# A decoder trunk's first chunk: the first weight block split ahead of the features' cast, the second tile's transposes ahead of all products, three warm-ups in place of six

## The chip, the core and the metric

The kernel runs on one core of one Trainium2 chip. The core has five engines with a queue of instructions each: TensorE (PE; its weight loads, which overlap its products, are listed as PEld), VectorE (DVE), ScalarE (ACT), GpSimd (POOL) and SyncE (SP). Each works through its own queue in order and meets the others at semaphores. Loads are issued from SP's queue here and carried out by 16 DMA engines. The metric is the time of one execution on the device in microseconds (us).

## What is computed

Two layers of a decoder trunk on 256 tokens of width 1024, all in float32. Each layer adds four things to the residual x: half of a SwiGLU feed-forward block, a mixer of two kinds of attention heads, a cross attention, and half of a second SwiGLU block. Only the first feed-forward block of the first layer is touched here:

```
def rms_norm(x, w):
    y = x * lax.rsqrt(jnp.mean(x * x, axis=-1, keepdims=True) + EPS)
    return y * w

def swiglu(h, w_gate, w_up, w_down):
    return (jax.nn.silu(h @ w_gate) * (h @ w_up)) @ w_down

x = x + 0.5 * swiglu(rms_norm(x, ffn1_norm[l]), ffn1_w_gate[l], ffn1_w_up[l], ffn1_w_down[l])
```

w_gate and w_up are 1024 x 2816, w_down is 2816 x 1024.

## The kernel before

**Products in three parts.** TensorE multiplies numbers of a reduced form of float32 (fp32r). Each operand is therefore split in two: a rounded part "hi" and the remainder "lo", and each product is made of three: hi x hi, hi x lo, lo x hi, summed in the same PSUM bank. For weights, ACT writes hi (tile whi) and DVE lo (tile wlo); in the blocks of this chunk ACT multiplies by the norm's gain on the way (L153) and DVE subtracts (L154). For features, the 256 tokens are two tiles of 128 rows. PE transposes a tile of x into PSUM (four transposes of 128 x 128 make one tile "pt"), ACT casts it to hi (xfh, L369), DVE makes lo (xfl, L370).

**The weight stream.** All weights come in one planned list of transfers of 1 MB each (raw). Raw 0 and raw 1 are the two halves (weight rows 0 to 511 and 512 to 1023) of the first 512 columns of w_gate, raw 2 and raw 3 those of w_up, raw 4 and 5 the next gate columns, raw 6 and 7 the next up columns. There are three buffers (`rawp`, bufs=3), so raw 3 loads into raw 0's buffer once that is split, raw 4 into raw 1's, and so on. `fetch` (L128) issues them on SP; raw 0 and raw 1 are issued in four pieces each, with the quarters of x between them. A raw block of this part holds four weight blocks of 128 rows x 512 columns, each split into one whi and one wlo. `split_block` splits a single block (and fetches two transfers ahead on its first); `take` and `split` do the same for whole transfers, one ahead of the products that read them.

**The first chunk.** `first_chunk` (L482) computes the first 512 gate columns from x without its norm: the norm's gain is in the weights and its row factor is applied later by the silu (`silu`, L704, two ACTIVATE with scale rs). x arrives in quarters (tile t, half b), and raw 0 in pieces, so that the work can start early. `turn(t, b)` is four transposes, `put(pt, t, b)` the cast and the remainder, `part(kt, t, which)` one product of 128 x 512 for weight block kt, tile t and one of the three kinds (0 is xfh x whi, 1 is xfh x wlo, 2 is xfl x whi), and `block(kt)` all six of a weight block. `warm_up(n)` is n transposes of the identity whose result nobody reads; nine of them stand at the very start as well (L232).

**Order.** The block is written inside `in_order()`, which ties each instruction to the one before it on the same engine: the order in the text is the order on every engine. After the block the order comes from the framework's scheduler, which goes by the order of the text and by what its model of time holds ready, and by a planner in the kernel (`drive`), whose tasks give their cost by `yield`.

**After it.** `xstat` computes the first 512 up columns from raw 2 and raw 3 (L442 to L444). Then `silu` and `mult` (L709, DVE, once per tile) give silu(gate) x up; a task (`h_task`, L693, eight transposes "hp") transposes that 2.4 planner microseconds later, while `wstat` has begun the second gate chunk from raw 4 and raw 5.

Of the kernel before, what the change touches and what calls it, by code (L numbers as in the profile page):

```python
# [24 lines left out]
NT = S // P  # L25
# [20 lines left out]
def hymba_kernel(  # L46
# [19 lines left out]
    def nm(s):  # L66
        uid[0] += 1
        return f"{s}_{uid[0]}"

    def s4(shape, dt=F32, name="s4"):  # L70
        return sp.tile(shape, dt, name=nm(name), tag="s4")

    def small(cols, name="sc", rows=P, bufs=0):
        return sm.tile([rows, cols], F32, name=nm(name), tag=name, bufs=bufs or 4)

    def acc(name="acc"):
        return psa.tile([P, 512], F32, name=nm(name), tag="acc")

    def smp(name="smp"):
        return pss.tile([P, 512], F32, name=nm(name), tag="smp")  # L80
# [48 lines left out]
    def fetch(i):  # L129
        while len(raws) <= min(i, len(plan) - 1):  # L130
            src, nk, cw, _ = plan[len(raws)]
            r = rawp.tile([P, 4 * 520], F32, name=nm("raw"), tag="raw")
            rv = r[:, :nk * cw].rearrange("p (k c) -> p k c", k=nk)
            n = 4 if len(raws) < 2 else 1
            for k0 in range(0, nk, nk // n):
                nc.sync.dma_start(out=rv[:, k0:k0 + nk // n, :], in_=src[:, k0:k0 + nk // n, :])
                for t, j in ({0: [(1, 0)], 3: [(0, 1), (1, 1)]}.get(k0, []) if not raws else []):
                    load_x(t, j)
            raws.append(r)
# [5 lines left out]
    def split_k(i, sl, k, hi, lo):  # L145

        gk = plan[i][3]
        if gk is None:
            nc.scalar.copy(out=hi, in_=sl)  # L149
            nc.vector.tensor_tensor(out=lo, in0=sl, in1=hi.bitcast(F32), op=ALU.subtract)  # L150
        else:
            g = gcols[gk[0]][:, gk[1] + k:gk[1] + k + 1]
            nc.scalar.mul(hi, sl, g)  # L153
            nc.vector.scalar_tensor_tensor(out=lo, in0=sl, scalar=g, in1=hi.bitcast(F32), op0=ALU.mult,  # L154
                                           op1=ALU.subtract)

    def split_block(i, k):

        if k == 0:
            fetch(i + LA_D - 1)  # L160
            pieces.append([])
        cw = plan[i][2]
        if k % 2 == 0:
            slot[:] = [wp.tile([P, SLOT], F32R, name=nm(n), tag=n) for n in ("whi", "wlo")]
        sl = slice(k % 2 * cw, (k % 2 + 1) * cw)
        hi, lo = slot[0][:, sl], slot[1][:, sl]
        split_k(i, raws[i][:, k * cw:(k + 1) * cw], k, hi, lo)
        pieces[i].append((hi, lo))
        return [(hi, lo)]
# [30 lines left out]
    @contextmanager  # L200
    def in_order():

        traced = nc.cur_bb.bb.instructions
        n = len(traced)
        yield
        prev = {}
        for i in traced[n:]:
            if i.engine in prev:
                tc.add_manual_dep(i, prev[i.engine], mybir.DependencyInfo(mybir.DependencyClass.NoSync,
                                  mybir.DependencyReason.DATA), reason="in_order")  # L210
            prev[i.engine] = i.name
# [13 lines left out]
    def warm_up(n):  # L225
        for i in range(n):
            nc.tensor.transpose(warm[:, (i % 4) * P:(i % 4 + 1) * P], ident, ident)
# [113 lines left out]
    def inv_rms(ss, rs):  # L341
        ms = small(1, "ms")
        nc.vector.scalar_tensor_tensor(out=ms, in0=ss[:, 0:1], scalar=EPS, in1=ss[:, 1:2], op0=ALU.add, op1=ALU.add)
        nc.gpsimd.tensor_tensor(out=rs, in0=ms, in1=neghalf[:, 0:1], op=ALU.pow)  # L344

    def half(ap, j):
        return ap[:, j * 512:(j + 1) * 512]
# [20 lines left out]
    def put_split(hi, lo, src):  # L368
        nc.scalar.copy(out=hi, in_=src)  # L369
        nc.vector.tensor_tensor(out=lo, in0=src, in1=hi.bitcast(F32), op=ALU.subtract)  # L370
# [79 lines left out]
    def xstat(f, cw, ps):  # L450
        ps += [acc() for _ in range(NT)]
        for kb in range(2):
            pc = take()
            for j in range(4):
                c = 0.0
                for t in range(NT):
                    c += xmm(ps, f, 4 * kb + j, t, pc[j], cw)
                yield c
# [23 lines left out]
    def first_chunk(f, psa_, psb_):  # L482


        psa_ += [acc(), acc()]
        rs = [small(1, "rs0", bufs=2) for _ in range(NT)]
        sq = [s4([P, D], F32, "sq") for _ in range(NT)]
        sums = [small(2, "ss") for _ in range(NT)]
        pa = []

        def turn(t, b):
            pt = smp("pt")
            for j in range(4):
                kt = 4 * b + j
                nc.tensor.transpose(pt[:, j * P:(j + 1) * P], xs[:, t, kt * P:(kt + 1) * P], ident)
            return pt

        def put(pt, t, b):
            sl = slice(t * P, (t + 1) * P)
            put_split(f.h[b][:, :, sl], f.l[b][:, :, sl], pt.rearrange("p (k t) -> p k t", k=4))  # L500

        def part(kt, t, which):
            x = (f.hi, f.hi, f.lo)[which](kt, t)
            w = (pa[kt][0], pa[kt][1], pa[kt][0])[which]
            nc.tensor.matmul(psa_[t], lhsT=x, rhs=w, start=kt == 0 and which == 0, stop=kt == KT - 1 and which == 1)  # L505

        def block(kt, order=(0, 2, 1)):
            first = order[:2] if order[1] == 2 else order[:1]
            for t in range(NT):
                for w in first:  # L510
                    part(kt, t, w)
            for w in order[len(first):]:
                for t in range(NT):
                    part(kt, t, w)

        def squares(t):
            x = xs[:, t, :]
            nc.scalar.activation(sq[t][:, 0:512], half(x, 0), AF.Square, scale=1.0 / 32.0, accum_out=sums[t][:, 0:1])
            nc.vector.tensor_tensor_reduce(out=sq[t][:, 512:1024], in0=half(x, 1), in1=half(x, 1), scale=1.0 / 1024.0,
                                           scalar=0.0, op0=ALU.mult, op1=ALU.add, accum_out=sums[t][:, 1:2])  # L520

        with in_order():
            p0 = turn(0, 0)
            warm_up(6)
            put(p0, 0, 0)
            pa += split_block(0, 0)
            part(0, 0, 0)
            part(0, 0, 2)
            p1 = turn(1, 0)
            put(p1, 1, 0)  # L530
            part(0, 0, 1)
            for w in (0, 2, 1):
                part(0, 1, w)
            for kt in (1, 2):
                pa += split_block(0, kt)
                block(kt)
            pa += split_block(0, 3)
            p = [turn(t, 1) for t in range(NT)]
            block(3)
            pa += split_block(1, 0)  # L540
            for t in range(NT):
                put(p[t], t, 1)
            block(4, (0, 1, 2))
            for kt in (5, 6, 7):
                pa += split_block(1, kt - 4)
                if kt < 7:
                    squares(kt - 5)
                block(kt)
            taken[0] = 2
            for t in range(NT):  # L550
                inv_rms(sums[t], rs[t])
        yield 16 * T512
        yield from xstat(f, 512, psb_)
        rb = sq[0].rearrange("p (j t) -> p j t", j=8)
        pt = smp("rt")
        for t in range(NT):
            nc.vector.tensor_scalar(out=rb[:, t, :], in0=ident, scalar1=0.0, scalar2=rs[t], op0=ALU.mult, op1=ALU.add)
            nc.tensor.transpose(pt[:, t * P:(t + 1) * P], rb[:, t, :], ident)
        row = sm.tile([P, S], F32, name=nm("L"), tag="L", bufs=1)
        nc.vector.tensor_copy(out=row, in_=pt[:, 0:S])  # L560
        hrs = [small(1, "hrs0", bufs=2) for _ in range(NT)]
        for t in range(NT):
            nc.vector.tensor_scalar(out=hrs[t], in0=rs[t], scalar1=0.5, scalar2=None, op0=ALU.mult)
        return rs, hrs, row
# [634 lines left out]
```

## Time and profile before

| | |
|---|---|
| median of three runs | 1235.88 us (1235.5 to 1235.89) |
| profiled execution, own time | 1236.02 us |
| profiled execution, span of instructions | 1234.2 us |
| PE busy | 1222.1 us of the span |
| DVE busy | 770.2 us |
| ACT busy | 653.7 us |
| HBM traffic | 217.28 MB read, 177 GB/s over the span |

The profile is of one execution. Its own time is a little longer than the span from its first to its last instruction. The views used below are the page (summary), the timeline (instructions in order of time: start, duration, engine, line, operation, output<-inputs, shape, number merged, and in brackets the idle time of the engine ahead of it with what ended it), the table of stretches (busy time of each engine in a stretch, then the granted TensorE clock, the DMA engines' busy share and their GB/s), the load table (size and us from issue to landing) and the waits (who waited for whom: us in total, times, longest). A time quoted from the timeline is counted from the span's start. Matmuls are pipelined, so one that lasts 0.39 us can follow another after 0.23.

### The profile page before, as it was taken

Reading aid. Unit: us, or ns where it says so; the run is one execution under the profiler, and the core shown is the slowest. Engines: PE = TensorE matmul, PEld = TensorE weight load, DVE = VectorE, ACT = ScalarE, POOL = GpSimd, SP = SyncE. Lnnn points to the kernel's source line nnn. Section 1 sums busy time; section 2 is a strip of 40 time slices with the busy share of each in tenths; the row PEclk is TensorE's granted clock in tenths of the full one; section 3 lists DMA queues with packets and bytes.
Section 4 is the critical chain, followed back from the end, with each engine's and each line's share of the span. In section 5 each row is a group of like instructions: output and inputs, shape, how many; then the busy total and the mean of one; then the engine's idle time right before and its main releaser. Section 6 shows DMA issues by size and latency. Waiting matters only on the chain.

```text
span 1234.2 us, 21594 instructions
## 1 busy us (share of the span) xinstructions
PE 1222.1 (99%) x9053; PEld 1118.8 (91%) x9053; DVE 770.2 (62%) x1190; ACT 653.7 (53%) x1022; POOL 36.6 (3%) x52
## 2 busy tenths in 40 slices
PE   9999999999999999999999999999999999999997
PEld 7999888999889889998889998889998898999986
DVE  6966647588866665554474464475887766545643
ACT  7655435578754454444354453366686555443532
POOL 0000000001000000000000000000010000000000
PEclk9999999999999999999999999999999999999999
DMA  8655655643544375465374566465434533555740
GB/s 309 208 182 175 242 185 172 216 143 109 184 157 154 116 243 173 171 224 191 130 256 144 199 205 204 136 222 189 154 139 171 187 134 106 195 181 171 239 170 35
DMA packets 100290, 219.73 MB, mean 178 GB/s; under 512 B 4160, under 2 KB 16736, under 8 KB 100192
## 3 DMA queue, kind: packets, MB, share of 16 engines
q1 hardware_dynamic: 100032, 218.07, 52.3%
q8 instruction: 71, 1.16, 0.4%
q10 hardware_dynamic: 160, 0.27, 0.1%
q14 instruction: 27, 0.22, 0.1%
HBM read 217.28 MB, written 1.05 MB: 177 GB/s over the span
## 4 chain that ended last, share of the span: by engine, by line
PE 93%; DVE 4%; ACT 1%; POOL 1%; issue 1%; DMA 0%; POOLq 0%; ACTq 0%
PE acc L442 29%; PE acc L443 29%; PE acc L444 28%; DVE wlo L150 1%; PE pt L363 1%; PE acc L505 1%; PE al L771 1%; DVE wlo L154 1%; DVE xfl L370 0%; POOL rs L344 0%; POOL hrs L840 0%; DVE pp L899 0%; PE cpo L443 0%; PE cs L442 0%; PE cs L444 0%
## 5 line engine op out<-in xcount | busy, mean ns | idle before, releaser
L150 DVE TENSOR_TENSOR wlo<-raw,whi 128x1024 fp32r<-128x1024 f32 (+1 forms) x324 | 388.6, 1222 | 270.4 <-ACT whi L149 269.4
L149 ACT CAST whi<-raw 128x1024 fp32r<-128x1024 f32 (+1 forms) x324 | 330.5, 1048 | 275.1 <-PE acc L444 134.6
L442 PE MATMUL acc<-xfh,whi 128*128 128x256 f32 x1536 | 432.4, 282 | 0.0
L443 PE MATMUL acc<-xfl,whi 128*128 128x256 f32 x1536 | 430.7, 280 | 0.3 <-DVE xfl L370 0.2
L444 PE MATMUL acc<-xfh,wlo 128*128 128x256 f32 x1536 | 429.8, 280 | 0.0
L443 PEld LDWEIGHTS acc<-xfl,whi 128*128 128x128 f32 x1536 | 289.3, 188 | 0.9 <-DVE xfl L370 0.7
L444 PEld LDWEIGHTS acc<-xfh,wlo 128*128 128x128 f32 x1536 | 289.4, 188 | 0.0
L442 PEld LDWEIGHTS acc<-xfh,whi 128*128 128x128 f32 x1536 | 288.5, 188 | 0.8
L443 PE MATMUL acc<-wlo,hth 128*128 128x512 f32 (+1 forms) x352 | 136.2, 387 | 0.0
L442 PE MATMUL acc<-whi,hth 128*128 128x512 f32 (+1 forms) x352 | 136.0, 386 | 0.0
L444 PE MATMUL acc<-whi,htl 128*128 128x512 f32 (+1 forms) x352 | 135.6, 385 | 0.0
L442 PE MATMUL acc<-whi,xfh 128*128 128x512 f32 (+1 forms) x240 | 87.8, 366 | 0.0
L443 PE MATMUL acc<-wlo,xfh 128*128 128x512 f32 (+1 forms) x240 | 87.3, 364 | 0.0
L444 PE MATMUL acc<-whi,xfl 128*128 128x512 f32 (+1 forms) x240 | 87.1, 363 | 0.0
L444 PEld LDWEIGHTS acc<-whi,htl 128*128 128x128 f32 x352 | 66.2, 188 | 14.1
L442 PEld LDWEIGHTS acc<-whi,hth 128*128 128x128 f32 x352 | 66.1, 188 | 14.2
L443 PEld LDWEIGHTS acc<-wlo,hth 128*128 128x128 f32 x352 | 66.1, 188 | 13.9
L154 DVE SCALAR_TENSOR_TENSOR wlo<-raw,g,whi 128x512 fp32r<-128x512 f32 (+1 forms) x96 | 62.0, 702 | 19.9 <-PE acc L444 11.4
L153 ACT ACTIVATE whi<-raw,g 128x512 fp32r<-128x512 f32 (+1 forms) x96 | 58.1, 677 | 18.1 <-PE acc L443 14.4
L369 ACT CAST hth<-sil 128x512 fp32r<-128x512 f32 x36 | 22.3, 619 | 56.8 <-DVE sil L738 56.8
L444 PEld LDWEIGHTS acc<-whi,xfl 128*128 128x128 f32 x240 | 45.1, 188 | 7.6
L442 PEld LDWEIGHTS acc<-whi,xfh 128*128 128x128 f32 x240 | 45.1, 188 | 7.6
(271 smaller groups left out, 1553.5 us busy)
## 6 DMA issues: line engine op xcount, KB each, us to landing
raw<-in_ffn_w_down_dram SPq DMA_DIRECT2D x44, 1024.0 KB, 4.9
raw<-in_ffn_w_up_dram SPq DMA_DIRECT2D x40, 1024.0 KB, 5.2
raw<-in_ffn_w_gate_dram SPq DMA_DIRECT2D x38, 1024.0 KB, 5.2
raw<-in_w_in_dram SPq DMA_DIRECT2D x24, 1024.0 KB, 5.3
raw<-in_cross_wk_dram SPq DMA_DIRECT2D x8, 1024.0 KB, 5.3
raw<-in_cross_wv_dram SPq DMA_DIRECT2D x8, 1024.0 KB, 5.1
raw<-in_w_out_dram SPq DMA_DIRECT2D x8, 1024.0 KB, 4.9
raw<-in_cross_wq_dram SPq DMA_DIRECT2D x8, 1024.0 KB, 5.0
```

What stands on the lines that cost most here:

```text
L149: nc.scalar.copy(out=hi, in_=sl)
L150: nc.vector.tensor_tensor(out=lo, in0=sl, in1=hi.bitcast(F32), op=ALU.subtract)
L153: nc.scalar.mul(hi, sl, g)
L154: nc.vector.scalar_tensor_tensor(out=lo, in0=sl, scalar=g, in1=hi.bitcast(F32), op0=ALU.mult, op1=ALU.subtract)
L363: nc.tensor.transpose(pt[:, j * P:(j + 1) * P], hn[:, kt * P:(kt + 1) * P], ident)
L369: nc.scalar.copy(out=hi, in_=src)
L442: nc.tensor.matmul(ps, lhsT=lh, rhs=rh, start=start, stop=False)
L443: nc.tensor.matmul(ps, lhsT=lh, rhs=rl, start=False, stop=False)
L444: nc.tensor.matmul(ps, lhsT=ll, rhs=rh, start=False, stop=stop)
L505: nc.tensor.matmul(psa_[t], lhsT=x, rhs=w, start=kt == 0 and which == 0, stop=kt == KT - 1 and which == 1)
L771: nc.tensor.matmul(ps[s0:s0 + hb, c0:c0 + hb], lhsT=k[:, h, a:a + hb], rhs=rhs[:, h, a + step:a + step + hb], start=True, stop=True)
```

## The change

Only the start of the ordered block in `first_chunk` is rewritten:

```
         with in_order():
             p0 = turn(0, 0)
-            warm_up(6)
+            pa += split_block(0, 0)
             put(p0, 0, 0)
-            pa += split_block(0, 0)
-            part(0, 0, 0)
-            part(0, 0, 2)
+            warm_up(3)
             p1 = turn(1, 0)
             put(p1, 1, 0)
-            part(0, 0, 1)
-            for w in (0, 2, 1):
-                part(0, 1, w)
+            for t in range(NT):
+                for w in (0, 1, 2):
+                    part(0, t, w)
             for kt in (1, 2):
                 pa += split_block(0, kt)
                 block(kt)
```

The split of weight block 0 (L153 on ACT, L154 on DVE, and the issue of raw 2 on SP, which it contains) comes ahead of the cast and remainder of tile 0. Three warm-up transposes stand between the two tiles' transposes in place of six. The second tile's transposes come ahead of all six products of block 0; two of these stood ahead of them, one right behind. The products then go tile by tile in the order hi x hi, hi x lo, lo x hi. Nothing is computed that was not computed before.

## The prediction

> **What bounds the kernel now.** I read the page first: shares of busy time, then the chain that ended last.
>
> ```profile
> span 1234.2 us, 21594 instructions
> PE 1222.1 (99%) x9053; PEld 1118.8 (91%) x9053; DVE 770.2 (62%) x1190; ACT 653.7 (53%) x1022; POOL 36.6 (3%) x52
> PE 93%; DVE 4%; ACT 1%; POOL 1%; issue 1%; DMA 0%; POOLq 0%; ACTq 0%
> ```
>
> PE is busy for 1222.1 of 1234.2 us, so all stages together leave it 12.1 us of idle time; the change touches code of the first chunk alone. A table of stretches (us; then busy time per engine, PE first) says how much of the idle time lies there.
>
> ```profile
> 0.00:10.00 10.00, 7.69 (x31) 5.95 (x32) 3.55 (x10) 4.50 (x7) 0.70 (x6) 1.00 0.78 271
> 10.00:20.00 10.00, 10.00 (x49) 8.22 (x48) 8.02 (x17) 7.63 (x15) 1.40 (x2) 1.00 1.00 368
> ```
>
> In the first 10 us PE idles 2.3, from 10 to 20 not at all. The timeline of the first 10 us (start, us, engine, line; in brackets the idle time ahead and what ended it) shows what the ten are spent on.
>
> ```profile
> 4.01 1.12 PE L495 MATMUL pt<-ident,xs 128*128 128x128 f32 x4 [0.27 <-DMA xs<-in_x_dram]
> 4.92 1.49 PE L227 MATMUL warm<-ident 128*128 128x128 f32 x6
> 5.17 0.59 ACT L369 CAST xfh<-pt 128x512 fp32r<-128x512 f32 x1 [2.53 <-PE pt L495]
> 5.65 0.72 ACT L153 ACTIVATE whi<-raw,g 128x512 fp32r<-128x512 f32 x1
> 6.41 0.75 DVE L154 SCALAR_TENSOR_TENSOR wlo<-raw,g,whi 128x512 fp32r<-128x512 f32 x1
> 6.43 0.80 PE L505 MATMUL acc<-whi,xfh 128*128 128x512 f32 x1
> 7.02 0.50 PE L505 MATMUL acc<-whi,xfl 128*128 128x512 f32 x1
> 7.35 0.60 PE L495 MATMUL pt<-ident,xs 128*128 128x128 f32 x4
> 7.99 0.58 ACT L369 CAST xfh<-pt 128x512 fp32r<-128x512 f32 x1 [1.62 <-PE pt L495]
> 8.47 2.57 ACT L153 ACTIVATE whi<-raw,g 128x512 fp32r<-128x512 f32 x4
> 8.61 0.69 DVE L370 TENSOR_TENSOR xfl<-pt,xfh 128x512 fp32r<-128x512 f32 x1 [1.45 <-ACT xfh L369]
> 9.23 2.74 DVE L154 SCALAR_TENSOR_TENSOR wlo<-raw,g,whi 128x512 fp32r<-128x512 f32 x4
> 9.35 0.50 PE L505 MATMUL acc<-whi,xfl 128*128 128x512 f32 x1 [0.22 <-DVE xfl L370]
> 9.69 0.39 PE L505 MATMUL acc<-wlo,xfh 128*128 128x512 f32 x1
> 9.92 0.39 PE L505 MATMUL acc<-whi,xfh 128*128 128x512 f32 x1
> ```
>
> The last row is the first product of weight block 1; from there the products start 0.23 us apart (9.69 to 9.92). Ahead of it stands one path: transposes, warm-ups, cast and split, two products, the second tile's transposes (7.35), their cast (7.99), their remainder (8.61), the product at 9.35.
>
> **The change part by part.** I rebuild that stretch in the new order with these durations. For arrivals I take the load table narrowed to one issue each (last figure: us from issue to landing): weight piece 0, issued at 1.18, then x tile 1, issued at 1.65.
>
> ```profile
> raw<-in_ffn_w_gate_dram SPq DMA_DIRECT2D x1, 256.0 KB, 3.4
> ```
> ```profile
> xs<-in_x_dram SPq DMA_DIRECT2D x1, 256.0 KB, 3.8
> ```
> ```profile
> 1.18 0.42 SPq L136 DMA_DIRECT2D raw<-in_ffn_w_gate_dram  x1
> 1.65 0.42 SPq L143 DMA_DIRECT2D xs<-in_x_dram  x1
> ```
>
> *Split first.* Piece 0 is there at 1.18 + 3.4 = 4.58, so ACT makes whi at about 4.6 instead of 5.65, into time in which it idles now (2.53 us ahead of the cast). Four splits take 2.57, so one follows another after (2.57 - 0.72) / 3 = 0.62; the cast of tile 0 comes at 5.25 instead of 5.17 and ends at 5.84. Cost 0.08, covered, since no product can use it before the second tile's transposes are through. On DVE wlo runs from 5.4, xfl of tile 0 from 6.05 to 6.75. SP's issue of the next raw block, inside the split, is only emitted earlier; its place on SP's queue is the same.
>
> *Three warm-ups fewer, transposes moved up.* The four transposes at 4.01 hold PE for 4.92 - 4.01 = 0.91 us until the first warm-up starts, 0.23 each; with three warm-ups of the same shape PE gets to the second tile's transposes at 4.92 + 3 x 0.23 = 5.6, not 7.35. x tile 1 lands at 1.65 + 3.8 = 5.45, hardly ahead of that. Four transposes as long as those at 4.01 (1.12) end at 6.72. PE's queue behind them now holds all products: the one that ran at 6.43 goes after 6.6. That costs nothing where it counts, since what comes last is tile 1's chain: cast 6.76 to 7.34 (0.04 behind PE, as at 7.99), xfl 7.38 to 8.07, its product 8.11. The other five products, with inputs from 7.34 or earlier, fit between 6.6 and 8.11. Block 1 follows 9.92 - 9.35 = 0.57 later in the old order with one product between; now the waiting one is last of six, and the next comes 9.69 - 9.35 = 0.34 later: 8.45. ACT splits block 1 from 7.3 to 8.0, DVE till 8.8, and that remainder is needed by its fifth product only, 0.9 behind 8.45. **Gain at this point: 9.92 - 8.45 = 1.5 us**; between 1.2 (the six products at a slow pace) and 1.8 (tile 1's transposes at the quick pace, 0.3 sooner).
>
> *What is late next.* PE is then ahead of the old times by 1.5, and I look for the first thing it meets that is not. Within the first chunk it could be raw 1: the row at 8.47 is raw 0's last three blocks and raw 1's first, which was there by 8.47 + 3 x 0.62 = 10.3 and is now wanted at 9.1. If it lands no sooner than 10.3, ACT waits and ends its split at 11.0, with the casts of x's other half queued behind it; but those need transposes that PE reaches at 8.45 + 2 x 6 x 0.23 = 11.2, so this costs nothing. The next views are ACT, DVE, PE's weight loads and PE, from 20 to 36 us.
>
> ```profile
> 21.35 2.57 ACT L153 ACTIVATE whi<-raw,g 128x512 fp32r<-128x512 f32 x4 [1.43 <-DMA raw<-in_ffn_w_up_dram]
> 23.94 1.28 ACT L704 ACT_TABLE_LOAD   x1
> 25.23 1.27 ACT L704 ACTIVATE sil<-acc,rs 128x512 f32<-128x512 f32 x2
> 26.39 7.46 ACT L153 ACTIVATE whi<-raw,g 128x512 fp32r<-128x512 f32 x12
> ```
> ```profile
> 29.87 3.39 DVE L154 SCALAR_TENSOR_TENSOR wlo<-raw,g,whi 128x512 fp32r<-128x512 f32 x5
> 33.18 0.68 DVE L709 TENSOR_TENSOR sil<-sil,acc 128x512 f32<-128x512 f32 x1
> ...
> 34.11 0.67 DVE L709 TENSOR_TENSOR sil<-sil,acc 128x512 f32<-128x512 f32 x1
> ```
> ```profile
> 34.44 0.19 PEld L444 LDWEIGHTS acc<-xfh,wlo 128*128 128x128 f32 x1
> ```
> ```profile
> 35.03 1.03 PE L693 MATMUL hp<-ident,sil 128*128 128x128 f32 x8
> ```
>
> ACT waits 1.43 us for raw 3 (second half of the first up chunk, 21.3), and from there on it has no pause, for PE or anything else: four splits, table load, two silus, twelve splits. DVE's remainders follow these: the row at 29.87 is raw 5's four and raw 6's first, and behind it come the two L709, which end at 34.78. The eight transposes at 35.03 read what the two L709 write, four each. Now the landing of raw 3: issue on SP's queue, its load time, and what SP waited for just ahead of it.
>
> ```profile
> 12.40 0.38 SPq L136 DMA_DIRECT2D raw<-in_ffn_w_up_dram  x1
> ```
> ```profile
> raw<-in_ffn_w_up_dram SPq DMA_DIRECT2D x1, 1024.0 KB, 8.9
> ```
> ```profile
> SPq L136 <- DMA raw<-in_ffn_w_gate_dram: 0.3, 1, 0.3
> ```
>
> 12.40 + 8.9 = 21.3. Its buffer is raw 0's, whose last split ends at 9.23 + 2.74 = 11.97, but SP's last wait is for another load to land, not for DVE. Freeing raw 0 by 1.5 us sooner therefore moves nothing here. So the chain raw 3, splits, silu, splits, L709 stays where it is, and PE runs into it. With 1.5 in hand it comes to L693 at 33.5: it waits to 33.18 + 0.68 + 0.05 = 33.91 for the first four (0.05 from DVE's end to PE's start, as at 9.35), and to 34.83 for the other four, which started at 35.03 + 4 x 0.11 = 35.46 in before (eight take 1.03 and the four at 7.35 took 0.60, so 0.11 each). **0.6 us of the 1.5 is left**, less some 0.1 for starting up again: 0.5. It is all the same then whether the first stretch brings 0.8 or 1.8. Between, the products of the second gate chunk need the last remainder of raw 5, ready at 29.87 + 3 x 0.66 + 0.75 = 32.6 (0.66 = (3.39 - 0.75) / 4); the row at 34.44 is the first load that reads it, now at 32.9: just in time. After L693 both orders are the same with PE 0.5 ahead. DVE and ACT have more idle time there (62% and 53% busy over the span), and weight buffers are freed by PE itself, so I let the 0.5 reach the end.
>
> **The sum.** The profiled execution took 1236.02 us, 1.8 more than its span and 0.14 above the median of 1235.88. Less 0.5 it gives 1235.5; from the median, 1235.4, which is my forecast.
>
> **The rivals.**
> *The whole shift goes through* (1.5 us: 1234.4). It needs the L709 sooner: if, with the first chunk's products ending 1.5 sooner, the program's scheduler places the silus (with table load 2.55 us) ahead of raw 3's splits, in the 1.43 + 1.5 us in which ACT has nothing; or if it places L709 ahead of the fifth split of the row at 29.87 (0.66). For it: this part of the order is not written by hand, and L709 stands behind a split of raw 6 now. Against: both depend on the same early block, so their order should be kept. 22%.
>
> *Raw 3 lands later: the slower one* (1236.8). Raw 4 may load once raw 1 is split, now 1.5 us sooner, and may then share the DMA engines with the end of raw 3.
>
> ```profile
> 18.47 0.38 SPq L136 DMA_DIRECT2D raw<-in_ffn_w_gate_dram  x1
> ```
> ```profile
> raw<-in_ffn_w_gate_dram SPq DMA_DIRECT2D x1, 1024.0 KB, 5.5
> ```
>
> At the 368 GB/s of 10 to 20 us 1 MB moves in 2.8 us, so raw 4 starts 5.5 - 2.8 = 2.7 us after its issue: now at 17.0 + 2.7 = 19.7. Raw 3 has 1.6 us to go then; evenly shared it would take 1.6 longer. L693's second half would come at 34.83 + 1.6 = 36.4 against 35.46, 0.9 late. It decides from 0.6 us of delay on. Against: the landings of the two single-issue rows come in order of issue (4.58, then 5.45), an earlier load ahead of a later one. [...] 10%.
>
> *PE's slow pace lasts longer* (1236.8). In before four transposes took 1.12 at 4.01 and 0.60 at 7.35, 0.23 against 0.11 apart, at a granted clock of 1.00 in both rows of stretches (third figure from the end): PE doubled its pace some 3.3 us after the transposes began. If it takes 3.3 us from the products on instead, which now begin at 6.7, each product from 8.45 to 10 costs 0.46 and not 0.23: 1.55 / 0.46 = 3.4 products, 0.8 us, which the wait at L693 hides (1.5 - 0.8 is still 0.7). If it takes twice that, to 13.3, it is 10.5 products and 2.4 us, and PE is 0.9 behind before for good. [...] 4%.
>
> That the change does not do what it says is excluded on its own engines' orders, since the block is ordered by hand; what the scheduler does with all that comes after is not, and could shift waits anywhere: 14%, of which 6 beyond 0.2% to either side.
>
> **How the numbers follow.** Forecast 50%: 1235.1 to 1235.7 (first stretch or restart otherwise by 0.3). Whole shift 22%: 1234.0 to 1234.6. Raw 3 late 10%: 1235.9 to 1236.8. Slow pace 4%. Range 1234.0 to 1236.8. 0.2% is 2.5 us, about what a measurement of this kernel can tell from no change; no case that I can price reaches it. So faster 0.06, same 0.88, slower 0.06.
>
> **What would show it.** Right: whi of block 0 at 4.6; second tile's transposes at 5.6; block 1's first product at 8.45; ACT's splits of raw 3 still from 21.3; and a new wait of PE's hp transposes for DVE's L709 of about 0.9 us in two pieces. Wrong: no such wait with raw 3 unmoved, the silus ahead of raw 3's splits, or a block 1 that starts after 9.3.

## The result and the profile after

The changed kernel takes 1238.99 us (median of 7 runs, 1238.4 to 1240.04); the kernel before took 1235.88 in the same measurement (7 runs, 1235.35 to 1236.93). The ratio is 1.0024, 95% interval 1.0015 to 1.0033: slower by 3.1 us, where 1235.4 was forecast and "slower by over 0.2%" had a chance of 0.06. The profiled execution took 1238.72 us.

The page of the changed kernel, span and busy time:

```profile
span 1236.9 us, 21588 instructions
PE 1224.1 (99%) x9050; PEld 1120.0 (91%) x9050; DVE 771.2 (62%) x1190; ACT 653.9 (53%) x1022; POOL 36.7 (3%) x52
```

Against before the span is 2.7 us longer and PE's busy time 2.0 us longer, so PE's idle time has grown by 0.7 only. The time is not lost in waits. First the place where the change was made, in the timeline of the first 10 us (start, duration, engine, line; lines behind the block are 2 less than before):

```profile
3.93 1.11 PE L495 MATMUL pt<-ident,xs 128*128 128x128 f32 x4 [0.19 <-DMA xs<-in_x_dram]
4.69 1.28 ACT L153 ACT_TABLE_LOAD   x1 [4.69 <-DMA raw<-in_ffn_w_gate_dram]
4.84 0.72 PE L227 MATMUL warm<-ident 128*128 128x128 f32 x3
5.98 0.72 ACT L153 ACTIVATE whi<-raw,g 128x512 fp32r<-128x512 f32 x1
6.61 0.57 ACT L369 CAST xfh<-pt 128x512 fp32r<-128x512 f32 x1
7.04 0.66 PE L495 MATMUL pt<-ident,xs 128*128 128x128 f32 x4 [1.47 <-DMA xs<-in_x_dram]
7.73 0.59 ACT L369 CAST xfh<-pt 128x512 fp32r<-128x512 f32 x1 [0.56 <-PE pt L495]
8.35 0.69 DVE L370 TENSOR_TENSOR xfl<-pt,xfh 128x512 fp32r<-128x512 f32 x1 [0.26 <-ACT xfh L369]
9.10 0.50 PE L505 MATMUL acc<-whi,xfl 128*128 128x512 f32 x1
9.44 0.40 PE L505 MATMUL acc<-whi,xfh 128*128 128x512 f32 x1
```

Two rows are later than forecast. whi of block 0 comes at 5.98 and not at 4.6: ACT's table load (1.28 us) stands ahead of its first activation and waits with it for weight piece 0 (4.69). In before the first activation was the cast, its table load carried no such wait and ran in ACT's empty time:

```profile
1.36 1.28 ACT L369 ACT_TABLE_LOAD   x1 [1.36 <-PEq L1186]
```

And the second tile's transposes come at 7.04 and not at 5.6, since PE waits 1.47 us for x tile 1. In the load table narrowed to that one issue (last figure: us to landing) it took 5.3 us, against 3.8 in before, from the same place in SP's queue:

```profile
xs<-in_x_dram SPq DMA_DIRECT2D x1, 256.0 KB, 5.3
```

Block 1's first product starts at 9.44: 0.48 sooner than before's 9.92, not 1.5. Next the chain into which PE was to run. SP's queue, the load of raw 3, then ACT, DVE and PE from 20 to 36 us:

```profile
12.45 0.38 SPq L136 DMA_DIRECT2D raw<-in_ffn_w_up_dram  x1
13.07 0.33 SPq L338 DMA_DIRECT2D wn<-in_cross_norm_dram  x1
```
```profile
raw<-in_ffn_w_up_dram SPq DMA_DIRECT2D x1, 1024.0 KB, 7.7
```
```profile
20.18 2.57 ACT L153 ACTIVATE whi<-raw,g 128x512 fp32r<-128x512 f32 x4 [0.74 <-DMA raw<-in_ffn_w_up_dram]
```
```profile
32.93 0.68 DVE L707 TENSOR_TENSOR sil<-sil,acc 128x512 f32<-128x512 f32 x1
34.59 1.03 PE L691 MATMUL hp<-ident,sil 128*128 128x128 f32 x8
```

The scheduler has put raw 3 ahead of the norm's weights (512 KB), which stood ahead of it in before. Raw 3 landed 1.2 us sooner (7.7 us from its issue, 8.9 in before), ACT's splits of it start at 20.18 and not 21.35, the second silu product ends at 33.61, and the hp transposes (L691 now) wait for nothing at 34.59. At that point PE is 0.44 us ahead of before (35.03).

From there the lead is lost a little with every product. The two programs issue the same products in the same order after the first chunk, so each can be compared with itself in the other trace. Here is its start in the changed kernel less its start in the kernel before, both counted from the span's start:

```
at us:     53    133   253   373   493   613   733   853   973   1093  1213  last
offset:  -0.39 -0.04 +0.28 +0.37 +0.58 +1.00 +1.55 +1.84 +1.98 +2.15 +2.58 +2.69
```

That is 3.1 us over some 8,900 products, 0.35 ns each, and the largest lasting step is 0.1 us. The groups of PE's costliest lines say the same (busy time in us, then mean ns of one); before, then after:

```profile
L442 PE MATMUL acc<-xfh,whi 128*128 128x256 f32 x1536 | 432.4, 282 | 0.0
L443 PE MATMUL acc<-xfl,whi 128*128 128x256 f32 x1536 | 430.7, 280 | 0.3 <-DVE xfl L370 0.2
L444 PE MATMUL acc<-xfh,wlo 128*128 128x256 f32 x1536 | 429.8, 280 | 0.0
```
```profile
L442 PE MATMUL acc<-xfh,whi 128*128 128x256 f32 x1536 | 433.5, 282 | 0.0
L443 PE MATMUL acc<-xfl,whi 128*128 128x256 f32 x1536 | 431.4, 281 | 0.4 <-DVE xfl L370 0.2
L444 PE MATMUL acc<-xfh,wlo 128*128 128x256 f32 x1536 | 430.4, 280 | 0.0
```

Same counts, idle time ahead of them of 0.3 and 0.4 us in all, and 1.1 + 0.7 + 0.6 = 2.4 us more in these three groups. A product that waits for nothing has become slower, in lines that the change doesn't touch.

What differs there was found in the built programs. Behind the first chunk the order of every engine is the same (but for raw 3's issue), the mean granted clock is 0.999 in both, and every buffer has its old address but one kind. The split weights live in seven places each, whi and wlo, that are given out in turn. In before both go through their seven in the turn 0 6 5 4 1 2 3; in the changed kernel whi still does, while wlo goes 0 6 5 1 2 3 4. Four of seven remainders thus lie at another place beside the same whi, to the end of the program. That is the suspicion which the experiments test: **theory A**, the places of wlo set the pace of the products; **theory B**, the order of the first chunk, or the state in which it leaves PE, does.

### The profile page after: what moved, and what is told of

It is laid out like the page before. It is cut to its first block, busy times and chain, and to the rows that moved or that the text cites. A ratio compares the mean times of both kernels' runs of the same rounds, so it can differ in the third digit from the quotient of the medians.

```text
span 1236.9 us, 21588 instructions
## 1 busy us (share of the span) xinstructions
PE 1224.1 (99%) x9050; PEld 1120.0 (91%) x9050; DVE 771.2 (62%) x1190; ACT 653.9 (53%) x1022; POOL 36.7 (3%) x52
## 4 chain that ended last, share of the span: by engine, by line
PE 94%; DVE 3%; POOL 1%; ACT 1%; issue 1%; DMA 0%; SPq 0%; POOLq 0%; ACTq 0%
PE acc L442 29%; PE acc L443 29%; PE acc L444 29%; PE pt L363 1%; PE acc L505 1%; DVE wlo L150 1%; PE al L769 1%; DVE wlo L154 1%; DMA xs<-in_x_dram 0%; POOL hrs L838 0%; DVE pp L897 0%; PE cpo L443 0%; PE cs L444 0%; PE cs L443 0%; PE cs L442 0%
## 5 line engine op out<-in xcount | busy, mean ns | idle before, releaser
L442 PE MATMUL acc<-xfh,whi 128*128 128x256 f32 x1536 | 433.5, 282 | 0.0
L443 PE MATMUL acc<-xfl,whi 128*128 128x256 f32 x1536 | 431.4, 281 | 0.4 <-DVE xfl L370 0.2
L444 PE MATMUL acc<-xfh,wlo 128*128 128x256 f32 x1536 | 430.4, 280 | 0.0
L443 PEld LDWEIGHTS acc<-xfl,whi 128*128 128x128 f32 x1536 | 289.3, 188 | 1.0 <-DVE xfl L370 0.8
L442 PEld LDWEIGHTS acc<-xfh,whi 128*128 128x128 f32 x1536 | 289.5, 188 | 0.7
L444 PEld LDWEIGHTS acc<-xfh,wlo 128*128 128x128 f32 x1536 | 289.5, 188 | 0.0
L442 PE MATMUL acc<-whi,hth 128*128 128x512 f32 (+1 forms) x352 | 136.3, 387 | 0.0
L443 PE MATMUL acc<-wlo,hth 128*128 128x512 f32 (+1 forms) x352 | 136.2, 387 | 0.0
L444 PE MATMUL acc<-whi,htl 128*128 128x512 f32 (+1 forms) x352 | 136.1, 387 | 0.0
L442 PE MATMUL acc<-whi,xfh 128*128 128x512 f32 (+1 forms) x240 | 88.0, 367 | 0.0
L443 PE MATMUL acc<-wlo,xfh 128*128 128x512 f32 (+1 forms) x240 | 87.3, 364 | 0.0
L444 PE MATMUL acc<-whi,xfl 128*128 128x512 f32 (+1 forms) x240 | 87.2, 364 | 0.0
L444 PEld LDWEIGHTS acc<-whi,htl 128*128 128x128 f32 x352 | 66.2, 188 | 14.4
L443 PEld LDWEIGHTS acc<-wlo,hth 128*128 128x128 f32 x352 | 66.2, 188 | 14.2
L442 PEld LDWEIGHTS acc<-whi,hth 128*128 128x128 f32 x352 | 66.2, 188 | 14.2
L154 DVE SCALAR_TENSOR_TENSOR wlo<-raw,g,whi 128x512 fp32r<-128x512 f32 (+1 forms) x96 | 62.1, 705 | 22.9 <-PE acc L444 15.0
L153 ACT ACTIVATE whi<-raw,g 128x512 fp32r<-128x512 f32 (+1 forms) x96 | 58.2, 677 | 19.2 <-PE acc L443 15.1
L369 ACT CAST hth<-sil 128x512 fp32r<-128x512 f32 x36 | 22.3, 619 | 57.9 <-DVE sil L736 57.9
L444 PEld LDWEIGHTS acc<-whi,xfl 128*128 128x128 f32 x240 | 45.2, 188 | 7.7
L442 PEld LDWEIGHTS acc<-whi,xfh 128*128 128x128 f32 x240 | 45.1, 188 | 7.5
```

The source lines that it names most:

```text
L442: nc.tensor.matmul(ps, lhsT=lh, rhs=rh, start=start, stop=False)
L443: nc.tensor.matmul(ps, lhsT=lh, rhs=rl, start=False, stop=False)
L444: nc.tensor.matmul(ps, lhsT=ll, rhs=rh, start=False, stop=stop)
```

## The experiments

For each kernel the number that tells most is the growth of that same offset against the kernel before, from 53 us to the last product; it leaves out what the first chunk itself does. The table collects them; the turns are those of places.

```
kernel                       whi turn       wlo turn       at 53 us  last   growth
changed kernel               0 6 5 4 1 2 3  0 6 5 1 2 3 4   -0.39   +2.69   +3.1
after_warm6                  0 6 5 4 1 2 3  0 6 5 1 2 3 4   -0.66   +2.63   +3.3
after_xfirst                 0 6 5 4 1 2 3  0 6 5 1 2 3 4   +2.77   +5.82   +3.0
after_forced                 0 6 5 4 1 2 3  0 6 5 1 2 3 4   +5.35   +8.32   +3.0
before_slots                 0 6 5 4 1 2 3  0 6 5 1 2 3 4   +6.22   +9.56   +3.3
after_lolast                 0 6 5 4 1 2 3  0 6 5 4 1 2 3   -0.49   -0.57   -0.1
lolast_xfirst_table          0 6 5 4 1 2 3  0 6 5 4 1 2 3   +1.07   +0.62   -0.5
lolast_xfirst_table_warm6    0 6 5 4 1 2 3  0 6 5 4 1 2 3   +0.08   +0.42   +0.3
after_slots                  0 6 5 4 1 2 3  0 6 5 4 1 2 3   +5.13   +5.42   +0.3
before_forced                0 6 5 4 1 2 3  0 6 5 4 1 2 3   +4.66   +4.75   +0.1
after_both                   0 6 5 1 2 3 4  0 6 5 1 2 3 4   +5.33   +5.03   -0.3
after_whi                    0 6 5 1 2 3 4  0 6 5 4 1 2 3   +4.96   +4.83   -0.1
after_rot                    0 6 5 4 1 2 3  6 5 4 1 2 3 0   +3.66   +7.25   +3.6
```

Single pauses set the scatter of this number: where both turns are the old ones it runs from -0.5 to +0.3, and of the -0.5 of lolast_xfirst_table nearly all falls at one place, where PE in before pauses for 0.30 us (858.99) and here does not.

### Places given by hand, in both kernels

In place of one pool of seven buffers for each kind, seven pools of one buffer, taken in a written turn:

```
-    wp = ctx.enter_context(tc.tile_pool(name="wp", bufs=N_W))
+    wps = {n: [ctx.enter_context(tc.tile_pool(name=f"{n}{k}", bufs=1)) for k in range(N_W)] for n in ("whi", "wlo")}
+    turns = {"whi": [0, 6, 5, 4, 1, 2, 3], "wlo": [0, 6, 5, 1, 2, 3, 4]}
+    used = {"whi": 0, "wlo": 0}
...
+    def wtile(n):
+        k = turns[n][used[n] % N_W]
+        used[n] += 1
+        return wps[n][k].tile([P, SLOT], F32R, name=nm(n), tag=n)
...
-                lo = wp.tile([P, SLOT], F32R, name=nm("wlo"), tag="wlo")
+                lo = wtile("wlo")
```

**after_slots**: the changed kernel, both turns equal.

> The kernel after, with each whi and wlo tile put by name into one of seven fixed places, and wlo's places taken in the turn of the kernel before (0 6 5 4 1 2 3, the same as whi's). Theory A (wlo's places set the pace of the products): the products lose no more time against the kernel before than in its first 35 us, where the kernel after was 0.45 us ahead, so about 1235.5 us. Theory B (the loss comes with the order of the first chunk or the place of PE's instructions): as the kernel after, 1238.5 to 1239.5.

**after_forced**: the changed kernel, its own turns.

> Control for the run with wlo's places exchanged: the kernel after in the same way of writing, whi in the turn 0 6 5 4 1 2 3 and wlo in its own turn of the kernel after, 0 6 5 1 2 3 4. Both theories: as the kernel after, 1238.5 to 1239.5; under theory A some 3.3 us above the run with equal turns, under theory B the same as it.

**before_slots**: the kernel before, with the turns of the changed one.

> The kernel before with fixed places, wlo's taken in the turn of the kernel after (0 6 5 1 2 3 4), nothing else of the change. Theory A: slower by the 3.1 us that the products lost, 1238.5 to 1239.5. Theory B: as the kernel before, 1235.5 to 1236.5.

**before_forced**: the kernel before, its own turns.

> Control: the kernel before with fixed places and both turns as it has them (0 6 5 4 1 2 3). Both theories: 1235.5 to 1236.5; under theory A 3 us below the run with exchanged turns, under theory B the same as it.

Measured on one chip, beside 1236.43 for the kernel before: after_slots 1241.24 (ratio 1.0039, 1.0027 to 1.0052), after_forced 1244.58 (1.0063, 1.0051 to 1.0076), before_slots 1245.14 (1.0069, 1.0057 to 1.0082), before_forced 1241.37 (1.0041, 1.0027 to 1.0055). The differences are those of theory A: the exchanged turn costs 3.3 us in the changed kernel (1244.58 - 1241.24) and 3.8 in the kernel before (1245.14 - 1241.37), while at equal places the order of the first chunk changes 0.1 us (1241.24 against 1241.37). In the two programs built from the kernel before, the transfers' buffers (raw) come in another turn as well; before_forced, with a growth of 0.1 us, shows that this costs the products nothing. Theory B has nothing for the 3.8 in a kernel whose first chunk is the old one.

All four lie 5 to 6 us above what was expected of them, and the table says where: at 53 us they are already late by 4.7 to 6.2 us. Written this way, the program's scheduler places raw 2's splits ahead of the casts of x's second half. ACT and PE in before_forced (lines are 7 more there):

```profile
15.09 2.56 ACT L160 ACTIVATE whi<-raw,g 128x512 fp32r<-128x512 f32 x4 [3.97 <-DMA raw<-in_ffn_w_up_dram]
17.55 1.04 ACT L376 CAST xfh<-pt 128x512 fp32r<-128x512 f32 x2
```
```profile
18.17 1.28 PE L512 MATMUL acc<-whi,xfh 128*128 128x512 f32 x2 [2.95 <-ACT xfh L376]
```

ACT waits 3.97 us for a load with work standing behind it that could run, and PE waits 2.95 us for that work. So these four settle the pace, but not the sum.

### The same engines' orders, with the places restored

**after_lolast**: one line of the changed kernel, which sets only the order of block 0's six products on PE.

```
             for t in range(NT):
-                for w in (0, 1, 2):
+                for w in (0, 2, 1):
                     part(0, t, w)
```

In the built program it restores wlo's old turn; the orders of the four other engines are exactly those of the changed kernel.

> The changed kernel with block 0's products in the order hi x hi, lo x hi, hi x lo instead of hi x hi, hi x lo, lo x hi; nothing else is edited. In the built program this puts the remainders' seven buffers back to the same turn of places as the rounded parts' (0 6 5 4 1 2 3 for both), at the places of the kernel before; only four instructions of block 0 stand in another order on TensorE. Theory A (the place of wlo sets the pace of the products that load it): the offset of the product times against the kernel before stays at about -0.4 us from 26 us to the end, so 1235.5 us, some 3.3 under the changed kernel, within 0.2% of the kernel before. Theory B (the order of the first chunk, or which state it leaves PE in, sets the later pace): as the changed kernel, 1239, ratio 1.0024, offset growing by 3 us.

Measured: 1236.63 us (11 runs) beside 1236.22 for the kernel before (27 runs on the same chip): ratio 1.0005, 0.9996 to 1.0014, no difference. The profiled execution has a span of 1233.6 us, 0.6 less than before. The offset stays where the first chunk leaves it (-0.49, at the end -0.57). The three groups of after_lolast are those of before to 0.1 us:

```profile
L442 PE MATMUL acc<-xfh,whi 128*128 128x256 f32 x1536 | 432.4, 282 | 0.0
L443 PE MATMUL acc<-xfl,whi 128*128 128x256 f32 x1536 | 430.6, 280 | 0.3 <-DVE xfl L370 0.2
L444 PE MATMUL acc<-xfh,wlo 128*128 128x256 f32 x1536 | 429.8, 280 | 0.0
```

With the hand-placed pair this shows theory A: the change as a reordering is worth nothing that can be measured, and the 3 us come with the places that the allocator deals out, which hang on the order in which the first remainders are read.

### What about the places counts

Three kernels as after_forced, with another line of turns each (in this order: **after_both**, **after_whi**, **after_rot**); one profile of each, read by its growth.

```
-    turns = {"whi": [0, 6, 5, 4, 1, 2, 3], "wlo": [0, 6, 5, 1, 2, 3, 4]}
+    turns = {"whi": [0, 6, 5, 1, 2, 3, 4], "wlo": [0, 6, 5, 1, 2, 3, 4]}
+    turns = {"whi": [0, 6, 5, 1, 2, 3, 4], "wlo": [0, 6, 5, 4, 1, 2, 3]}
+    turns = {"whi": [0, 6, 5, 4, 1, 2, 3], "wlo": [6, 5, 4, 1, 2, 3, 0]}
```

> The changed kernel with fixed places, both turns exchanged alike (whi and wlo both 0 6 5 1 2 3 4). Read by the offset of the product times against the kernel before, 40 us against the last product; the fixed places' own 5 us lie ahead of that. Theory A1 (what counts is whether a wlo lies at the same place as its whi): no growth, as with both turns natural (+0.3). Theory A2 (wlo's own turn is a slow one, whatever whi does): growth of 3.1 us. Theory A3 (each combination of places of the weights that follow one another has a pace of its own): some other number.

> The changed kernel with fixed places, the turn of whi exchanged (0 6 5 1 2 3 4) and that of wlo natural (0 6 5 4 1 2 3): the mirror of the changed kernel. Growth of the offset from 40 us to the end: theory A1 (unequal places cost) +3 us; theory A2 (wlo's own turn) 0; theory A3 some other number, of either sign.

> The changed kernel with fixed places, wlo one step on in the same turn (whi 0 6 5 4 1 2 3, wlo 6 5 4 1 2 3 0): all seven pairs unequal instead of four of seven. Growth of the offset from 40 us to the end: theory A1 (unequal places cost) 7/4 of 3.1, 5.4 us; theory A2 (wlo's own turn) 0; theory A3 some other number, of either sign.

Measured: growth -0.3, -0.1 and +3.6 us (one execution each, of 1241.06, 1240.86 and 1243.28 us; 5.3, 5.0 and 3.7 of these are the lateness at 53 us that comes with the hand-given places). A1 (unequal places cost) falls by after_whi, which is as unequal as the changed kernel and costs nothing in sum, and by after_rot, which had 5.4 to come. A2 (wlo's turn as such) falls by after_both, where the changed kernel's turn of wlo costs nothing, and by after_rot, where the old turn, one step on, costs most. What is left is A3, that each combination has a pace of its own. The spacing of single products, worked out from the traces with the places from the built programs, fits it: for the products that load the weights and stream 256 columns of features, the mean of three spacings in a row (to L443, to L444, to the next L442), by the places of whi and wlo, is

```
before:   0,0 353.7   1,1 349.5   2,2 353.9   3,3 351.1   4,4 355.6   5,5 352.9   6,6 353.8 ns
changed:  0,0 354.2   1,2 352.6   2,3 358.9   3,4 350.8   4,1 356.6   5,5 352.2   6,6 353.9 ns
```

The three pairs that are the same in both kernels keep their spacing to 0.7 ns; of the four others three are slower beside the same whi, by 3.1, 5.0 and 1.0 ns, and one is faster by 0.3. With some 230 such threes to each pair that is 2.0 us of the 3.1; the rest lies in products of other shapes. No turn that was tried is faster than the old one by more than 0.3 us.

The traces of the other kernels bear A3 out. The changed kernel's seven numbers come again, to 0.2 ns, in after_forced and before_slots, whose first chunks differ. In after_both, with the pairs in another order, the seven equal pairs keep before's pace to 1.1 ns, and in after_rot the pair 2,3 is slow again (357.7). The pair isn't all: 0,0 takes 356.4 in after_whi. There these products lose 1.5 us in all, and products that stream the weights instead of loading them win 1.6 back, so that kernel's growth of nothing is a sum of two effects. The rule behind these numbers stays open.

### The first chunk: table load, arrival, warm-ups

**after_xfirst**: the changed kernel with x tile 1 issued ahead of weight piece 0.

```
+                if not raws and k0 == 0:
+                    load_x(1, 0)
...
-                for t, j in ({0: [(1, 0)], 3: [(0, 1), (1, 1)]}.get(k0, []) if not raws else []):
+                for t, j in ({3: [(0, 1), (1, 1)]}.get(k0, []) if not raws else []):
```

> The changed kernel with the first half of x tile 1 issued ahead of weight piece 0, and no early table load. x tile 1 at about 4.6 and so the second tile's transposes at 5.6 instead of 7.04; weight piece 0 at about 5.4, then the table load of 1.28 us on ACT ahead of the first split: whi at 6.7, wlo at 7.4, cast of tile 0 at 7.3, of tile 1 at 8.0, its remainder at 8.6. If the table load behind the wait is what holds the stretch, block 1's first product comes at about 9.3, no more than 0.1 us sooner than in the changed kernel; if x tile 1 alone held it, at 8.4. Time 1238.9 or 1238.0, against 1239.0.

Measured: 1241.52 us, ratio 1.0040 (1.0025 to 1.0056), 2.5 us above the changed kernel's own time; neither forecast. ACT, then PE:

```profile
6.17 1.28 ACT L155 ACT_TABLE_LOAD   x1 [6.17 <-DMA raw<-in_ffn_w_gate_dram]
7.46 0.72 ACT L155 ACTIVATE whi<-raw,g 128x512 fp32r<-128x512 f32 x1
```
```profile
8.71 0.80 PE L507 MATMUL acc<-whi,xfh 128*128 128x512 f32 x1 [1.84 <-ACT xfh L371]
...
12.78 0.63 PE L507 MATMUL acc<-whi,xfl 128*128 128x512 f32 x1
13.20 0.95 PE L507 MATMUL acc<-wlo,xfh 128*128 128x512 f32 x2
14.00 0.40 PE L507 MATMUL acc<-whi,xfh 128*128 128x512 f32 x1
```

Weight piece 0 lands at 6.17 instead of 4.69, the table load and the split add their 1.28 and 0.72, and PE has no product until 8.71. From there products start 0.43 us apart, where the changed kernel's are 0.23 apart, until about 13.6. At 53 us this kernel is 3.2 us behind the changed one.

**after_warm6**: the changed kernel with six warm-ups.

```
-            warm_up(3)
+            warm_up(6)
```

> The changed kernel with six warm-ups again instead of three; places of all buffers as in the changed kernel. By its trace PE finished the three warm-ups at about 5.6 and waited until 7.04 for x tile 1, so three more (0.23 us each, 0.7 us) fit into that wait: block 1's first product at 9.4 as before the edit, 1239.0 us. The rival is that the warm-ups set the clock of what follows: then the products of blocks 0 and 1 run at the quick pace earlier and the time falls by up to 0.5 us. If x tile 1 lands sooner on this occasion (3.8 us from issue, 5.45), the six warm-ups cost up to 0.7 us there.

Measured: 1238.71 us, ratio 1.0019 (1.0010 to 1.0028): as the changed kernel. The six cost nothing, as expected, for in this execution too PE waited for x tile 1:

```profile
6.33 0.66 PE L495 MATMUL pt<-ident,xs 128*128 128x128 f32 x4 [0.42 <-DMA xs<-in_x_dram]
```

Here it landed 4.6 us after its issue; with 3.8, 5.3 in the two kernels' traces and 5.1 in after_lolast's, the arrival of that one load differs by 1.5 us between executions of kernels that issue it at the same time. By these arrivals, taking three warm-ups out could gain only where the load is at its quickest; no run of a changed kernel shows that case.

**lolast_xfirst_table**: after_lolast with x tile 1 ahead and the table load brought forward by a small copy on ACT.

```
+    nc.scalar.copy(out=neghalf, in_=neghalf)
```

> As the run above, with two more edits: the first half of x tile 1 is issued ahead of weight piece 0 instead of behind it, and a one-column ACT copy early in the program brings the table load (1.28 us) forward into ACT's first idle time. Both theories of the later pace as above. The first chunk: x tile 1 at about 4.6, weight piece 0 at about 5.4, whi at 5.5 (5.98 in the changed kernel), second tile's transposes at 5.6, block 1's first product at 8.4 to 8.6 instead of 9.44: 0.9 us gained, unless PE is then at its slow pace when it starts on the products. If theory A holds and the later chains (raw 3, silu) give the time back, 1235.4; if they do not, 1234.5. If theory B holds, 1238.

Measured: 1237.35 us, ratio 1.0006 (0.9997 to 1.0015). whi came at 5.60 and the second tile's transposes at 5.69, both as expected, and yet the kernel is 1.1 us behind before at 53 us. PE:

```profile
5.69 1.06 PE L498 MATMUL pt<-ident,xs 128*128 128x128 f32 x4
...
8.78 0.63 PE L508 MATMUL acc<-whi,xfh 128*128 128x512 f32 x1
9.21 0.63 PE L508 MATMUL acc<-whi,xfl 128*128 128x512 f32 x1
...
11.77 0.73 PE L508 MATMUL acc<-wlo,xfh 128*128 128x512 f32 x2
12.34 0.40 PE L508 MATMUL acc<-whi,xfh 128*128 128x512 f32 x1
```

Products stand 0.43 us apart until 11.77 and 0.23 from there. Everything arrived in time and PE did the products at half pace, which is the case that the expectation names behind "unless".

**lolast_xfirst_table_warm6**: the same with six warm-ups.

> As the run with x tile 1 ahead, the early table load and the other order of products (1237.35; there the products of the first blocks stood 0.43 us apart from 6.84 to 11.77, PE having paused from 6.54 to 6.84 and from 7.3 to 7.76), but with six warm-ups, so that PE has no pause between the first transposes and the first product. [...] Theory G2 (with x tile 1 that early PE starts on the products before its pace has doubled, whatever it does ahead of them): 0.43 apart until 11 or 12 again, 1237.4.

```profile
5.37 1.49 PE L229 MATMUL warm<-ident 128*128 128x128 f32 x6
6.65 1.06 PE L498 MATMUL pt<-ident,xs 128*128 128x128 f32 x4
7.45 0.79 PE L508 MATMUL acc<-whi,xfh 128*128 128x512 f32 x1
8.36 0.80 PE L508 MATMUL acc<-whi,xfl 128*128 128x512 f32 x1
8.95 0.51 PE L508 MATMUL acc<-wlo,xfh 128*128 128x512 f32 x1
9.30 0.40 PE L508 MATMUL acc<-whi,xfh 128*128 128x512 f32 x1
```

Measured: 1236.30 us beside 1236.01 for the kernel before, ratio 1.0003 (0.9994 to 1.0013). The pace doubles at about 8.95, 2.8 us sooner than with three warm-ups, and at 53 us the kernel is level with before (+0.08) instead of 1.1 behind. That is against G2, by which the products would have stood 0.43 apart until 11 or 12 again. Weight piece 0 took 4.5 us to land here, and the kernel comes out level with before, not ahead of it. With one execution of each and different arrivals, what brought the doubling sooner is not shown. No kernel that was run is faster than the kernel before by anything that these measurements can tell.

## Why the prediction was wrong, point by point

**The path through the first chunk** (gain 1.5 us at block 1): 0.48 came. Two terms were mis-sized. whi was taken at 4.6 with ACT idle ahead of it; the table load that ran at 1.36 stood ahead of the cast (L369), the first activation of before, and when the split (L153) became the first, its 1.28 us moved behind weight piece 0: 5.98. And x tile 1's landing was taken as 3.8 us from the one execution shown; 5.3, 5.1 and 4.6 were measured since. In the profiled execution the second hides most of the first: tile 1's transposes at 7.04 lead to the product at 9.10. The chain from there is as forecast (from transposes to block 1: 8.45 - 5.6 = 2.85 us forecast, 9.44 - 7.04 = 2.40 measured, the transposes being at the quick pace).

**Raw 3 fixed at 21.3, and the new wait at the hp transposes**: wrong. SP's queue was not left alone: raw 3 went ahead of the norm's weights and its splits began at 20.18. There is no wait for L707. I had the right kind of doubt (14% for what the scheduler does elsewhere), but argued from a last wait of SP that nothing would move. The 11.97 beside it was misread too: the row at 9.23 ends with raw 1's first remainder, so raw 0's buffer was done with about 0.66 sooner; nothing in the sum hung on it.

**0.5 us left behind L693**: 0.44 to 0.48 measured, from a smaller gain and no wait in place of a larger gain and a wait. The number was right and its working was not. The 0.1 for starting up again in that sum was the author's estimate, which no run shows: at the hp transposes PE did not wait in the changed kernel.

**"After L693 both orders are the same with PE 0.5 ahead ... so I let the 0.5 reach the end"**: this step failed, and it alone carries the result. The orders are the same; the addresses are not. The lead of 0.44 turns into a lag of 2.69 at 0.35 ns a product, because the remainders of the weights lie in another turn of places. after_lolast, with the same orders on DVE, ACT, POOL and SP and the old turn, keeps its lead (-0.57 at the last product), and the kernel before with the new turn loses 3.3. With the old places the forecast of no measurable change would have held: 1.0005 (0.9996 to 1.0014).

**The rivals.** The whole shift did not go through, and raw 3 came sooner, not later. The slow pace, given 4%, did not come in the changed kernel (its second transposes took 0.66 for four), but in two kernels that bring x tile 1 ahead it did, for about 5 us each, from 6.84 to 11.77 and from 8.71 to 13.6, and in after_forced for 3.4. The 3.3 us that it was priced with, from the transposes at 4.01 to the quick ones at 7.35, did not come again: in the changed kernel the clock's first rise, at 5.31, stands 1.4 us behind the transposes at 3.93. The case that decided was none of the priced ones. No view of the profile of before shows the place of a buffer, so it could not be priced from there; as an unknown it should have been let into the range with both signs.

**Open**: by what rule the places act; and why after_lolast's executions spread from 1235.46 to 1238.78 while its profiled one is the lowest. The 3.0 to 3.3 us of growth are from profiled executions; the medians of after_lolast and after_warm6, from one chip, differ by 2.1.

## What to carry to other kernels

When a change is small and the trace drifts a little with every instruction (here 0.35 ns a product) instead of stepping once, compare the programs' buffer addresses before looking for a wait: here a reordering at the start shifted the turn in which the allocator deals out buffers, for the whole run. Watch which activation is the program's first: the table load (1.28 us) stood ahead of it in each of these kernels. With the cast first it ran at 1.36 us (before); with the split first it waited for weight piece 0, to 4.69 and 6.17 (the changed kernel, after_xfirst); a tiny activation early put it back to 1.36 (lolast_xfirst_table). Bringing products forward gained nothing in lolast_xfirst_table, where TensorE was still at its slow pace (products 0.43 us apart until 11.77): look at the spacing of the products as well as at when they start.

## What the runs showed of the hardware

**Places.** In the traces of before and of the changed kernel three products of 256 columns take 349.5 to 358.9 ns together, by the places of whi and wlo, with 0.3 and 0.4 us of idle time ahead of those products in all. With the turns of the changed kernel five kernels grew by 3.0 to 3.3 us to the last product, 0.25%, twice the 1.5 us that the change was to gain at block 1.

**Two paces.** In these traces PE's products of 128 x 512 start 0.23 us apart (before, 9.69 to 9.92) or 0.43 us apart (lolast_xfirst_table, 8.78 to 9.21) where nothing holds them. At the start of a program the granted clock of the stretches does not show it: lolast_xfirst_table from 8 to 10 us, with products 0.43 apart, has 1.00 (third figure from the end):

```profile
8.00:10.00 2.00, 2.00 (x5) 1.58 (x6) 2.00 (x4) 1.22 (x2) 0.00 (x0) 1.00 0.97 339
```

The records of that clock in the traces begin only with its first rise to full, and the table counts the time ahead of it as 1.00. That rise stands at 7.24 us in before, at 5.31 in the changed kernel, at 11.99 in lolast_xfirst_table, at 13.91 in after_xfirst and at 9.18 in lolast_xfirst_table_warm6, each time where the spacing changes.

After a pause later on the table shows it too. before_forced, behind the 2.95 us in which PE waited:

```profile
18.00:20.00 2.00, 1.83 (x4) 1.46 (x5) 2.00 (x4) 2.00 (x6) 0.00 (x0) 0.50 0.97 311
```

In after_forced PE was at the quick pace for its second transposes, lost it and had it back:

```profile
6.44 0.66 PE L502 MATMUL pt<-ident,xs 128*128 128x128 f32 x4 [1.06 <-DMA xs<-in_x_dram]
7.63 0.50 PE L512 MATMUL acc<-whi,xfh 128*128 128x512 f32 x1 [0.53 <-ACT xfh L376]
7.97 0.48 PE L512 MATMUL acc<-wlo,xfh 128*128 128x512 f32 x1
8.55 0.79 PE L512 MATMUL acc<-whi,xfl 128*128 128x512 f32 x1
...
11.70 0.43 PE L512 MATMUL acc<-whi,xfl 128*128 128x512 f32 x1
11.97 0.62 PE L512 MATMUL acc<-wlo,xfh 128*128 128x512 f32 x2
```

It was slow from between 7.97 and 8.55 to between 11.70 and 11.97, for 3.2 to 4.0 us; the clock's records have the fall at 8.36 and the rise at 11.77, 3.41 apart, and in before_forced at 17.80 and 21.21, 3.41 apart again. What sets these times no run shows: PE's first transpose starts at 1.36 in before and in the changed kernel, and the first rise of the clock came at 7.24 in the one and at 5.31 in the other. A rise came behind transposes alone, too: in after_warm6 PE had done nothing but transposes when the pace doubled, within its six warm-ups:

```profile
4.80 1.10 PE L227 MATMUL warm<-ident 128*128 128x128 f32 x6
```

The same six took 1.49 us in before; here they stand 0.21 us apart up to 5.23 and 0.11 from 5.41, with the rise of the clock at 5.38.
